# Conditioning products in halves for each head, and the second block's narrow heads in plain float32

## The chip, the cores and the metric

One core of one Trainium2 chip runs the whole program in one launch. Its engines are TensorE (matrix products), VectorE, ScalarE, GpSimd and the DMA queues. The metric is the device time of the core in microseconds (us), median over runs.

## The reference

The network has two blocks, each of two layers, in float32. The program keeps the product of float32 matrices by splitting each operand into a high part (float32r, a reduced format that TensorE reads in one pass) and a low part that holds the rest.

```python
def first_block(...):                    # 256 tokens, 256 context tokens, width 1024
    sc, sc_ctx = silu(c), silu(c_ctx)
    for l in range(2):                   # shift, scale, gate = split(sc @ w_ada + b_ada, 3)
        x, ctx = hybrid_layer(...)       # mlstm (4 heads), diff attention (8 heads), fourier; then merge

def second_block(...):
    for i in range(2):
        h = rms_norm(x, g_mix[i])
        x = x + (mixer_ab(h, ...) if i % 2 == 0 else mixer_cd(h, ...))
        x = x + memory_cross_attention(rms_norm(x, g_xq[i]), rms_norm(mem, g_mem[i]), ...)
        x = x + swiglu(rms_norm(x, g_ffn[i]), w_gate_up[i], w_down[i])
    return rms_norm(x, g_final)
```

mixer_ab has two attentions of 8 query and 2 key heads of 64 (normed and rotated; the second with a window and a sink). mixer_cd has one with 8 heads, 96 wide in scores and 64 in values (from low-rank projections), and a neighbourhood attention of 8 heads of 64 with a bias.

## The kernel before

Weights come in pieces of 512 KB. `weights` loads a piece on the sync queue into one of three `w_raw` buffers; ScalarE casts it to `w_high` (line 256); VectorE or GpSimd subtracts to give `w_low` (line 257), three buffers each. A product of split operands, `mm3`, is three float32r products, high by high, low by high and high by low (lines 262 to 264). Data are split in the same way: `split` (lines 270 and 271, or 273 and 274 with a scale), `stack_q` and `stack_k` (279 to 287), which lay the two parts of a 64-row operand one above the other in 128 rows, so that two products do (`mm_stacked`, 303 and 304).

The table `POOL` says, for each part of the program, which low parts of weights GpSimd makes: (1, 0), as for `ab`, is all of them, (3, 1), as for `cd`, each third, (0, 0) none.

The first block (to 1663 us of the profile) works on 512 tokens, in the later stages of layer 1 on 256. It is built in a block whose instruction order on every engine is set by a simulated timeline. In it stand the conditioning products sc @ w_ada: eight groups of 512 columns, `ada_product`, each with four raw pieces and eight plain float32 products of 32 stationary columns (line 510) into four column groups of one bank, the first four starting the sum and the last four ending it. Their pieces come through the same three `w_raw` buffers and the same queue as the weights. They stand behind heads 1 and 3 of the mlstm in both layers, and behind each pair of heads of the second attention in layer 0.

The second block's order is that in which the code is written, with the framework's filling in of work that is ready: mixer_ab (from 1663 us) does the key and value projection, two query projections (`tok_wide`, four pieces each), norm and rotation on VectorE (lines 330 to 348 and 1330 to 1348), transposes (1394, 1426), then for four pairs of heads and two kinds the scores, the softmax (`softmax_t`: maximum 1279, exponential 1286, scaling 1299, transposes 1301, split `p` 270 and 271) and the values (`pair_values`), which give `y` split again. The memory's keys and values (`memory_now`) for the cross attention are filled in between. The output projection (`residual`) follows. mixer_cd (from 2062 us) is made likewise with `near_project` for its second attention.

Of the kernel before, what the change touches and what calls it, by code (L numbers as in the profile page):

```python
# [30 lines left out]
SECOND = dict(load=2, act=16, q=8, p=4, x=4, e=3, s=2, t=3, r=2)  # L31
# [3 lines left out]
            merge0=(0, 0), merge1=(0, 0), t=(4, 2), e=(0, 0), ab=(1, 0), x=(3, 2), cd=(3, 1), f=(0, 0))  # L35
# [166 lines left out]
class Build:  # L202
# [97 lines left out]

    def mm_stacked(self, out, q, k, start=True, stop=True):
# [89 lines left out]
    def run(self):  # L391
        tc, nc = self.tc, self.nc
        with tc.tile_pool(name="sbuf", bufs=1) as base, \
# [19 lines left out]
            with tc.tile_pool(name="second", bufs=1, reuse_waits="tile") as self.pool, \  # L413
                    tc.tile_pool(name="psum2", bufs=1, space=PSUM) as self.ps:
                self.bufs, self.banks = SECOND, BANKS_2
                self.make_zeroed(4)
# [235 lines left out]
    def hybrid(self, l):  # L652
# [11 lines left out]
        for hd in range(4):  # L664
# [14 lines left out]
            if hd in (1, 3):  # L679
                self.ada_group(l, range(4 + hd // 2, 5 + hd // 2))  # L680
# [593 lines left out]
    def softmax_t(self, ps2, pts, qi, sink=None, row_scale=None):  # L1274
# [28 lines left out]
        if whole:  # L1303
# [62 lines left out]
    def mixer_ab(self, l):  # L1366
# [9 lines left out]
        for t in range(2):  # L1376
            kx = self.u("x")[:, :256]
            nc.scalar.activation(kx, pss[t][:, :256], AF.Copy, scale=r[:, t:t + 1])
            v = tuple(self.u("act", dt=F32R) for _ in range(2))
            vsrc = pss[t][:, 256:].rearrange("p (g c) -> p g c", c=64)  # L1380
            for dup in range(2):
                o = [x.rearrange("p (g u c) -> p g u c", u=2, c=64)[:, :, dup] for x in v]
                self.split(o[0], o[1], vsrc, scale=r[:, t:t + 1])
# [4 lines left out]
            kr = self.u("x")[:, :256]  # L1388
            kv = kr.rearrange("p (g c) -> p g c", c=64)
            self.rope_tok(kv[:, 0:2], ka, tab["r2_c"][:, t], tab["r2_s"][:, t], 2, 32)  # L1390
            self.rope_tok(kv[:, 2:4], kb, tab["r1_c"][:, t], tab["r1_s"][:, t], 2, 32)

            for g in range(4):
                nc.tensor.transpose((kt_ps, kt_ps2)[g // 2][:64, (g % 2) * S + t * P:(g % 2) * S + (t + 1) * P], kv[:, g], self.ident)
        kT = []
        for src in (kt_ps, kt_ps2):
            k = self.u("act", dt=F32R), self.zeroed()
            self.stack_k(k, src[:64])
            kT.append(k)
# [13 lines left out]
        for kind in range(2):  # L1413
# [14 lines left out]
            for i in range(2):  # L1428
                qT[kind].append([self.u("q", dt=F32R) for _ in range(2)])
                for u in range(2):  # L1430
                    self.stack_q(qT[kind][i][u], ptq[i][64 * u:64 * u + 64])
        for pr in range(4):
            for kind in range(2):
                g = pr // 2
                pts = self.new_pts()
                for qi in range(2):
                    ps = self.bank("sc").rearrange("p (u c) -> p u c", u=2)
                    qsl = slice((pr % 2) * S + qi * P, (pr % 2) * S + (qi + 1) * P)
                    ksl = slice(g * S, (g + 1) * S)
# [6 lines left out]
                def vs(u, s, g=g, kind=kind):  # L1446
                    lo = (2 * kind + g) * P
                    return tuple(x[:, lo:lo + 64 * (u + 1)] for x in vv[s])

                self.pair_values(y, 4 * kind + pr, pts, vs)  # L1450
# [3 lines left out]
    def near_project(self, pr, rb):  # L1454

        qk = []
        for j in range(2):
            w = self.weights("w_in_cd_2", 0, 0, KT, _cols(416 + 512 * j + P * pr, P))
            ps = self.feat(w, 0, self.h, 0, S)
            t = self.u("x")[:, :S]  # L1460
            self.nc.vector.tensor_tensor(t, ps, rb, op=ALU.mult)
            for u in range(2):
                if j == 0:
                    q = self.u("q", dt=F32R)[:, :S]
                    self.stack_q(q, t[64 * u:64 * u + 64])
                    qk.append(q)
                else:
                    k = self.u("q", dt=F32R)[:, :S], self.zeroed()[:, :S]
                    self.stack_k(k, t[64 * u:64 * u + 64])
                    qk.append(k)  # L1470
        return qk

    def mixer_cd(self, l):
# [5 lines left out]
        def values():  # L1479
            pss = self.tok_wide(arr, 0, h, _cols(416 + 1024, 512))  # L1480
            vd = []
            for t in range(2):
                v = tuple(self.u("act", dt=F32R) for _ in range(2))
                self.split(v[0], v[1], pss[t], scale=r[:, t:t + 1])
# [4 lines left out]
        for lo, n, gain in ((0, 2, "g_cq"), (256, 1, "g_ckv")):  # L1489
# [9 lines left out]
            c = tuple(self.u("p", [P, 2, S], F32R) for _ in range(2))  # L1499
# [42 lines left out]
        for t in range(2):  # L1542
# [7 lines left out]
            v = tuple(self.u("act", dt=F32R) for _ in range(2))  # L1550
            self.split(v[0], v[1], ps)
            vc.append(v)
        y = self.new_y2()
        for pr in range(4):
            pair = []
            for u in range(2):
# [8 lines left out]
            pts = self.new_pts()  # L1565
            for qi in range(2):
                ps = self.bank("sc").rearrange("p (u c) -> p u c", u=2)
                for u in range(2):
                    a, b = pair[u]
                    qsl = slice(qi * P, (qi + 1) * P)  # L1570
                    self.mm3(ps[:, u], (a[:, 0, qsl], b[:, 0, qsl]), (a[:, 1], b[:, 1]), True, True)
                self.softmax_t(ps, pts, qi)
            self.pair_values(y, pr, pts, lambda u, s, pr=pr: tuple(x[:, P * pr:P * pr + 64 * (u + 1)] for x in vc[s]))

            pts = self.new_pts()
            for qi in range(2):
# [11 lines left out]
            self.pair_values(y, 4 + pr, pts, lambda u, s, pr=pr: tuple(x[:, P * pr:P * pr + 64 * (u + 1)] for x in vd[s]))  # L1588
# [46 lines left out]
    def ffn(self, l):  # L1635
# [4 lines left out]
        for f in range(NF):  # L1640
# [11 lines left out]
            a = self.u("act" if f < 16 else "q", [P, 2, S], F32R)  # L1652
# [106 lines left out]
```

## Time and profile before

| | us |
|---|---|
| median of 3 runs | 2439.83 (2437.66 to 2440.39) |
| profiled execution | 2442.6 |
| its span | 2440.8 |
| TensorE busy | 2296.8 (94%) |
| VectorE busy | 1617.7 (66%) |
| ScalarE busy | 1163.4 (48%) |
| GpSimd busy | 472.2 (19%) |

The mean granted TensorE clock is 0.977 of full speed. A product's row shows it from its start to its end, and the next one starts before that end; what a product costs is read from the starts of two that follow each other.

### The profile page before, as it was taken

The page shows a single profiled execution, that of the slowest core. Times are in us where ns is not written, and L with a number is a line of the kernel's source. Part 1 is how long each engine was busy: PE and PEld are TensorE (multiplying, and loading weights), DVE is VectorE, ACT ScalarE, POOL GpSimd, SP SyncE. Part 2 cuts the span into 40 slices and gives each one's busy share as a digit, 9 for nine tenths or more (in the row PEclk, how much of TensorE's full clock was granted, in tenths as well). Part 3 has the DMA queues.
Part 4 walks back from the last instruction along what each step waited for, and adds up shares of the span by engine and source line. Part 5 has one row for each costly group of instructions (what it writes and reads, how often), then busy time and mean ns, then how long its engine had stood idle before and what let it go on. Part 6 is the DMA issues. An engine that isn't in the chain of part 4 may idle for free.

```text
span 2440.8 us, 40377 instructions
## 1 busy us (share of the span) xinstructions
PE 2296.8 (94%) x15566; PEld 2066.6 (85%) x15566; DVE 1617.7 (66%) x3372; ACT 1163.4 (48%) x2172; POOL 472.2 (19%) x354
## 2 busy tenths in 40 slices
PE   6999999999999999989999999898698999888998
PEld 3787878798797887779889999896588999788998
DVE  5745566466575555586557778666987766887765
ACT  3344443444554233335445666444465444665543
POOL 2422220111121102002110000123352211222221
PEclk8999999999999999999999999998899999999999
DMA  6223234323323434443445434554233555433554
GB/s 254 78 92 114 95 109 155 125 88 101 116 93 131 151 103 154 142 130 117 134 147 186 131 113 141 180 166 147 86 102 123 183 183 180 132 109 121 189 183 139
DMA packets 111072, 330.87 MB, mean 136 GB/s; under 512 B 12320, under 2 KB 24352, under 8 KB 110880
## 3 DMA queue, kind: packets, MB, share of 16 engines
q1 hardware_dynamic: 90432, 299.87, 37.5%
q10 hardware_dynamic: 20448, 28.42, 3.4%
q8 instruction: 123, 2.02, 0.4%
q14 instruction: 69, 0.57, 0.1%
HBM read 309.36 MB, written 18.87 MB: 134 GB/s over the span
## 4 chain that ended last, share of the span: by engine, by line
PE 80%; DVE 12%; ACT 3%; DMA 3%; issue 2%; POOL 0%; ACTq 0%; SPq 0%; DVEq 0%; POOLq 0%
PE mm L262 22%; PE mm L263 22%; PE mm L264 22%; PE pv L262 2%; PE pv L263 2%; PE pv L264 2%; DVE w_low L257 1%; DVE h L274 1%; ACT w_high L256 1%; DVE e L1299 1%; DMA w_raw<-wstream 1%; PE mm L510 1%; PE sc L303 1%; DVE mx L1279 1%; PE sc L304 1%
## 5 line engine op out<-in xcount | busy, mean ns | idle before, releaser
L256 ACT CAST w_high<-w_raw 128x1024 fp32r<-128x1024 f32 (+1 forms) x490 | 508.0, 1038 | 583.1 <-PE mm L263 351.8
L257 DVE TENSOR_TENSOR w_low<-w_raw,w_high 128x1024 fp32r<-128x1024 f32 (+1 forms) x395 | 497.3, 1260 | 189.3 <-ACT w_high L256 184.8
L262 PE MATMUL mm<-big,w_high 128*128 128x512 f32 (+1 forms) x1664 | 573.3, 346 | 12.4 <-DVE g L942 5.7
L263 PE MATMUL mm<-big,w_high 128*128 128x512 f32 (+1 forms) x1664 | 571.3, 344 | 0.0
L264 PE MATMUL mm<-big,w_low 128*128 128x512 f32 (+1 forms) x1664 | 570.0, 343 | 0.0
L257 POOL TENSOR_TENSOR w_low<-w_raw,w_high 128x1024 fp32r<-128x1024 f32 x95 | 230.4, 2428 | 739.6 <-ACT w_high L256 600.3
L262 PEld LDWEIGHTS mm<-big,w_high 128*128 128x128 f32 x1664 | 316.1, 190 | 56.6 <-DVE g L942 6.1
L264 PEld LDWEIGHTS mm<-big,w_low 128*128 128x128 f32 x1664 | 316.4, 190 | 37.5 <-DVE w_low L257 0.4
L263 PEld LDWEIGHTS mm<-big,w_high 128*128 128x128 f32 x1664 | 316.6, 190 | 36.5 <-DVE big L271 0.2
L263 PE MATMUL mm<-w_low,big 128*128 128x256 f32 x960 | 269.9, 282 | 4.2 <-POOL w_low L257 2.8
L262 PE MATMUL mm<-w_high,big 128*128 128x256 f32 x960 | 268.0, 282 | 1.6 <-ACT w_high L256 1.6
L264 PE MATMUL mm<-w_high,big 128*128 128x256 f32 x960 | 268.3, 281 | 0.0
L263 PE MATMUL mm<-h,w_high 128*128 128x256 f32 x896 | 255.5, 285 | 4.8 <-DVE h L274 4.1
L262 PE MATMUL mm<-h,w_high 128*128 128x256 f32 x896 | 253.4, 284 | 2.7 <-ACT h L273 1.7
L264 PE MATMUL mm<-h,w_low 128*128 128x256 f32 x896 | 253.6, 283 | 0.0
L263 PEld LDWEIGHTS mm<-w_low,big 128*128 128x128 f32 x960 | 181.1, 189 | 6.2 <-POOL w_low L257 3.7
L262 PEld LDWEIGHTS mm<-w_high,big 128*128 128x128 f32 x960 | 180.6, 189 | 3.5 <-ACT w_high L256 2.8
L264 PEld LDWEIGHTS mm<-w_high,big 128*128 128x128 f32 x960 | 181.0, 189 | 0.4
L263 PEld LDWEIGHTS mm<-h,w_high 128*128 128x128 f32 x896 | 169.7, 189 | 7.6 <-DVE h L274 7.5
L262 PEld LDWEIGHTS mm<-h,w_high 128*128 128x128 f32 x896 | 169.5, 190 | 4.4 <-ACT h L273 2.8
L264 PEld LDWEIGHTS mm<-h,w_low 128*128 128x128 f32 x896 | 169.7, 190 | 0.1
L1649 POOL TENSOR_TENSOR x<-x,r 128x256 f32<-128x256 f32 x44 | 60.2, 1368 | 190.7 <-ACT t L1648 190.7
(475 smaller groups left out, 4388.8 us busy)
## 6 DMA issues: line engine op xcount, KB each, us to landing
w_raw<-wstream SPq DMA_DIRECT2D x486, 512.0 KB, 3.4
w_raw<-wstream SPq DMA_DIRECT2D x32, 448.0 KB, 3.2
big<-wstream SPq DMA_DIRECT2D x16, 512.0 KB, 9.0
gates<-y ACTq DMA_DIRECT2D x24, 256.0 KB, 2.0
w<-gates SPq DMA_DIRECT2D x18, 256.0 KB, 3.8
load<-yacc ACTq DMA_DIRECT2D x16, 256.0 KB, 3.0
yacc<-w ACTq DMA_DIRECT2D x12, 256.0 KB, 2.0
gates<-y ACTq DMA_DIRECT2D x24, 128.0 KB, 1.8
```

Source lines behind the costliest of these rows:

```text
L256: nc.scalar.copy(h, raw)
L257: eng.tensor_tensor(lo, raw, h.bitcast(F32), op=ALU.subtract)
L262: nc.tensor.matmul(out, a[0], b[0], start=start, stop=False)
L263: nc.tensor.matmul(out, a[0], b[1], start=False, stop=False)
L264: nc.tensor.matmul(out, a[1], b[0], start=False, stop=stop)
L274: nc.vector.scalar_tensor_tensor(lo, src, scale, h.bitcast(F32), op0=ALU.mult, op1=ALU.subtract)
L303: nc.tensor.matmul(out, q, k[0], start=start, stop=False)
L304: nc.tensor.matmul(out, q, k[1], start=False, stop=stop)
L510: nc.tensor.matmul(ps[j:j + 32], self.sc32[:, 2 * q + k], raw[:, k], start=(q < 2), stop=(q >= 2))
L1279: nc.vector.reduce_max(mx, ps2, axis=AX.X, negate=True)
L1299: nc.vector.tensor_scalar(p[:, u], p[:, u], sm[:, u:u + 1], None, op0=ALU.mult)
L1649: nc.gpsimd.tensor_tensor(g, g, rb, op=ALU.mult)
```

## The change

The conditioning products are cut in two: `ada_half` loads two raw pieces and makes four products, one in each column group, each a sum of its own. The first half is copied to an SBUF buffer (`acc`) by ScalarE; in the second VectorE adds the buffer to the bank where ScalarE copied the bank. A half stands behind each head, sixteen in all. They have high priority, and the product that reads the last piece is put first, the other three behind it.

In the second block, scores and values of the heads of 64 and 96 are single plain float32 products. Queries, keys, probabilities and values there are not split; keys get two zero-padded tiles, one for each half of 128 rows, values stand between columns of zeros, so that both heads of a pair sum in one bank of 128 rows (four products for a pair where twelve were). `POOL` is (0, 0) for `ab` and `cd`: all low parts there are VectorE's. Buffers follow: `act` 8 for 16, four of `vz`, `p` 3 for 4.

```diff
-SECOND = dict(load=2, act=16, q=8, p=4, x=4, e=3, s=2, t=3, r=2)
+SECOND = dict(load=2, act=8, vz=4, q=8, p=3, x=4, e=3, s=2, t=3, r=2)
...
-            merge0=(0, 0), merge1=(0, 0), t=(4, 2), e=(0, 0), ab=(1, 0), x=(3, 2), cd=(3, 1), f=(0, 0))
+            merge0=(0, 0), merge1=(0, 0), t=(4, 2), e=(0, 0), ab=(0, 0), x=(3, 2), cd=(0, 0), f=(0, 0))
...
-    def ada_group(self, l, groups):
-        for g in groups:
-            self.ada_product(l, g)
...
-    def ada_product(self, l, g):
+    def ada_half(self, l, g, half):
 
         nc = self.nc
         ps = self.mm()
-        for q in range(4):
-            raw = self.raw_weights("w_ada", l, 2 * q, 2, _cols(512 * g, 512)).rearrange("p (k c) -> p k c", k=2)
-            for k in range(2):
-                j = 32 * (2 * (q % 2) + k)
-                nc.tensor.matmul(ps[j:j + 32], self.sc32[:, 2 * q + k], raw[:, k], start=(q < 2), stop=(q >= 2))
+        raw = [self.raw_weights("w_ada", l, 4 * half + 2 * q, 2, _cols(512 * g, 512)).rearrange("p (k c) -> p k c", k=2) for q in range(2)]
+
+        def product(j):
+            return nc.tensor.matmul(ps[32 * j:32 * j + 32], self.sc32[:, 4 * half + j], raw[j // 2][:, j % 2], start=True, stop=True)
+
+
+        with self.tc.high_priority():
+            first = product(3)
+            with self.tc.issue_after(first.ins if hasattr(first, "ins") else first):
+                for j in range(3):
+                    product(j)
+        if half == 0:
+            nc.scalar.copy(self.acc, ps)
+            return
         row = self.u("y")
-        nc.scalar.copy(row, ps)
+        nc.vector.tensor_tensor(row, ps, self.acc, op=ALU.add)
         pt = self.bank("tp")[:, :8]
...
-            if hd in (1, 3):
-                self.ada_group(l, range(4 + hd // 2, 5 + hd // 2))
+            self.ada_half(l, 4 + hd // 2, hd % 2)
...
+                if l == 0:
+                    self.ada_half(1, pair, u)
                 self.merge_gates(GATES_B)
-            if l == 0:
-                self.ada_group(1, range(pair, pair + 1))
...
+        if not isinstance(pts, tuple):
+            nc.scalar.copy(pts[:, :, :, sl], pt)
...
-    def pair_values(self, y, k, pts, vs):
-
-        po = self.bank("pv").rearrange("p (u c) -> p u c", u=2)
+    def between_zeros(self, n):
+
+        v = self.u("vz", [P, 64 * (2 * n + 1)])
+        self.nc.gpsimd.memset(v[:, :P * n].rearrange("p (g c) -> p g c", c=P)[:, :, :64], 0.0)
+        self.nc.gpsimd.memset(v[:, P * n:], 0.0)
+        return v, v[:, 64:].rearrange("p (g c) -> p g c", c=P)[:, :, :64]
+
+    def pair_values(self, y, k, pts, v, heads):
+
+        po = self.bank("pv")[:, :S]
         for u in range(2):
-            m = 64 * (u + 1)
+            lo = P * heads[u] + 64 * (1 - u)
             for s in range(2):
-                vh, vl = vs(u, s)
-                self.mm3(po[:m, u], (vh, vl), (pts[0][:, u, s], pts[1][:, u, s]), s == 0, s == 1)
-            rows = slice(64 * u, 64 * u + 64)
-            self.split(y[0][rows, k, :S], y[1][rows, k, :S], po[rows, u])
+                self.nc.tensor.matmul(po, v[s][:, lo:lo + P], pts[:, u, s], start=u == 0 and s == 0, stop=u == 1 and s == 1)
+        self.split(y[0][:, k, :S], y[1][:, k, :S], po)
...
-            v = tuple(self.u("act", dt=F32R) for _ in range(2))
-            vsrc = pss[t][:, 256:].rearrange("p (g c) -> p g c", c=64)
-            for dup in range(2):
-                o = [x.rearrange("p (g u c) -> p g u c", u=2, c=64)[:, :, dup] for x in v]
-                self.split(o[0], o[1], vsrc, scale=r[:, t:t + 1])
+            v, at = self.between_zeros(4)
+            nc.scalar.activation(at, pss[t][:, 256:].rearrange("p (g c) -> p g c", c=64), AF.Copy, scale=r[:, t:t + 1])
...
-                qT[kind].append([self.u("q", dt=F32R) for _ in range(2)])
-                for u in range(2):
-                    self.stack_q(qT[kind][i][u], ptq[i][64 * u:64 * u + 64])
+                qT[kind].append(self.u("q"))
+                nc.scalar.copy(qT[kind][i], ptq[i])
...
                     for u in range(2):
-                        self.mm_stacked(ps[:, u], qT[kind][pr // 2][u][:, qsl], tuple(x[:, ksl] for x in kT[kind]), kind == 0, kind == 0 or u == 1)
+                        nc.tensor.matmul(ps[:, u], qT[kind][pr // 2][:, qsl], kT[kind][g][u], start=kind == 0, stop=kind == 0 or u == 1)
...
+            if j == 0:
+                q = self.u("q")[:, :S]
+                self.nc.vector.tensor_tensor(q, ps, rb, op=ALU.mult)
+            else:
+                k = self.zeroed()
+                for u in range(2):
+                    sl = slice(64 * u, 64 * u + 64)
+                    self.nc.vector.tensor_tensor(k[u][sl], ps[sl], rb[sl], op=ALU.mult)
+        return q, k
...
-                a, b = (self.u("q", [P, 2, S], F32R)[:96] for _ in range(2))
-                self.split(a, b, pt)
-                pair.append((a, b))
-            pts = self.new_pts()
+                a = self.u("q", [P, 2, S])[:96]
+                nc.scalar.copy(a, pt)
+                pair.append(a)
...
-                    self.mm3(ps[:, u], (a[:, 0, qsl], b[:, 0, qsl]), (a[:, 1], b[:, 1]), True, True)
+                    nc.tensor.matmul(ps[:, u], pair[u][:, 0, qi * P:(qi + 1) * P], pair[u][:, 1], start=True, stop=True)
...
-                    self.mm_stacked(ps[:, u * S:(u + 1) * S], qk[u][:, qi * P:(qi + 1) * P], qk[2 + u])
+                    nc.tensor.matmul(ps[:, u * S:(u + 1) * S], qk[0][:, qi * P:(qi + 1) * P], qk[1][u], start=True, stop=True)
```

TensorE in the first block, around the group behind the first pair of heads of the second attention in layer 0; `big` and `sc_..<-k` are data of that attention, `w_raw` the conditioning weights. Before (the last pair of products, on the fourth piece, follows after four more score rows):

```order
L510 MATMUL mm_4436<-w_raw_4437,sc_13_97 32x512 x2
L510 MATMUL mm_4436<-w_raw_4441,sc_13_97 32x512 x2
L347 MATMUL tp_4089<-ones_64,e_4087 128x2 x4
L303 MATMUL sc_4208<-k_3627,q_3640 128x256
L304 MATMUL sc_4208<-kz_80,q_3640 128x256
L303 MATMUL sc_4213<-k_3631,q_3643 128x256
L1156 MATMUL tp_4199<-ident_62,e_4181 128x128 x2
L304 MATMUL sc_4213<-kz_74,q_3643 128x256
L510 MATMUL mm_4436<-w_raw_4445,sc_13_97 32x512 x2
```

After, the first half, behind the first head of that pair:

```order
L312 MATMUL sc_3944<-k_3611,q_3623 128x256
L313 MATMUL sc_3944<-kz_78,q_3623 128x256
L262 MATMUL mm_4063<-big_223,w_high_4059 128x512
L514 MATMUL mm_4114<-w_raw_4117,sc_13_97 32x512
L514 MATMUL mm_4114<-w_raw_4115,sc_13_97 32x512 x2
L514 MATMUL mm_4114<-w_raw_4117,sc_13_97 32x512
L263 MATMUL mm_4063<-big_224,w_high_4059 128x512
L264 MATMUL mm_4063<-big_223,w_low_4060 128x512
L262 MATMUL mm_4063<-big_223,w_high_4059 128x512
```

The products of a group stood in pairs, one for each piece, between other work; now the four of a half stand together, inside a projection's stream.

TensorE in mixer_ab, at the first scores of the second kind (`kz` are keys, `q` queries, `s` and `r` the window and the unit matrix, `mm` a projection of the memory). Before:

```order
L1426 MATMUL tp_18006<-ident_62,x_18009 128x128 x2
L1426 MATMUL tp_18005<-ident_62,x_18022 128x128 x2
L1426 MATMUL tp_18006<-ident_62,x_18022 128x128 x2
L1441 MATMUL sc_18108<-s_17769,r_17767 128x512
L303 MATMUL sc_18108<-act_17762,q_18033 128x256
L304 MATMUL sc_18108<-kz_17562,q_18033 128x256
L263 MATMUL mm_18620<-h_18581,w_high_18616 128x256
L264 MATMUL mm_18620<-h_18581,w_low_18617 128x256
```

After, with the values (`pv`) of a pair behind them:

```order
L1461 MATMUL sc_18102<-s_17797,r_17795 128x512
L1463 MATMUL sc_18102<-kz_17586,q_18053 128x256
L1314 MATMUL tp_18068<-ident_62,e_18064 128x128 x4
L1463 MATMUL sc_18102<-kz_17587,q_18053 128x256
L1314 MATMUL tp_18086<-ident_62,e_18082 128x128 x4
L1461 MATMUL sc_18126<-s_17797,r_17795 128x512
L1463 MATMUL sc_18126<-kz_17586,q_18053 128x256
L1463 MATMUL sc_18126<-kz_17587,q_18053 128x256
L1340 MATMUL pv_18094<-p_18057,vz_17692 128x256
L1340 MATMUL pv_18094<-p_18057,vz_17740 128x256
L1340 MATMUL pv_18094<-p_18057,vz_17692 128x256
L1340 MATMUL pv_18094<-p_18057,vz_17740 128x256
```

Two float32r products per score became one plain product, and the values of a pair are four products; the projections of the memory stand between them as before, with more of them ahead.

VectorE in mixer_ab, at the norm of the first keys (`hn`). Before:

```order
L274 SCALAR_TENSOR_TENSOR h_17568<-xres_17253,vecs_60,h_17568 128x256 x6
L274 SCALAR_TENSOR_TENSOR act_17669<-mm_17603,rstd_17588,act_17668 128x4x64
L1345 TENSOR_REDUCE hn_ss_17676<-t_17674 128x2
L334 TENSOR_SCALAR hn_r_v_17679<-hn_ss_17676 128x2
L335 TENSOR_SCALAR hn_r_y_17681<-hn_r_v_17679 128x2
L337 SCALAR_TENSOR_TENSOR hn_r_t_17680<-hn_r_y_17681 128x2
L338 TENSOR_TENSOR hn_r_t_17680<-hn_r_t_17680,hn_r_v_17679 128x2
L339 SCALAR_TENSOR_TENSOR hn_r_y_17681<-hn_r_t_17680,hn_r_y_17681 128x2
```

After:

```order
L274 SCALAR_TENSOR_TENSOR h_17592<-xres_17269,vecs_60,h_17592 128x256 x6
L257 TENSOR_TENSOR w_low_17668<-w_raw_17665,w_high_17667 128x1024
L257 TENSOR_TENSOR w_low_17808<-w_raw_17805,w_high_17807 128x1024
L257 TENSOR_TENSOR w_low_17826<-w_raw_17823,w_high_17825 128x1024
L1372 TENSOR_REDUCE hn_ss_17698<-t_17696 128x2
L343 TENSOR_SCALAR hn_r_v_17701<-hn_ss_17698 128x2
L344 TENSOR_SCALAR hn_r_y_17703<-hn_r_v_17701 128x2
L346 SCALAR_TENSOR_TENSOR hn_r_t_17702<-hn_r_y_17703 128x2
L347 TENSOR_TENSOR hn_r_t_17702<-hn_r_t_17702,hn_r_v_17701 128x2
L348 SCALAR_TENSOR_TENSOR hn_r_y_17703<-hn_r_t_17702,hn_r_y_17703 128x2
```

The split of the values (line 274 with `act`) is gone from there, and low parts of weights (257), which GpSimd made, stand ahead of the norm.

## Rows read from the trace of the kernel before

**Rows 1.** Engines busy, by stretch: first block; mixer_ab, its start; mixer_cd's attention.

```profile
core 0: us, PE busy (x) PEld busy (x) DVE busy (x) ACT busy (x) POOL busy (x), PEclk, DMA share, GB/s
0.00:1663.40 1663.40, 1589.75 (x10237) 1398.62 (x10237) 1053.48 (x2363) 756.27 (x1403) 270.64 (x222) 0.99 0.40 132
1663.40:1803.60 140.20, 107.97 (x552) 88.80 (x553) 113.36 (x259) 71.53 (x170) 48.13 (x21) 0.87 0.28 94
1663.40:1741.00 77.60, 56.62 (x224) 44.33 (x225) 57.03 (x127) 31.53 (x56) 28.99 (x12) 0.81 0.36 121
...
2106.00:2178.70 72.70, 61.16 (x442) 55.68 (x441) 59.89 (x119) 54.38 (x144) 15.41 (x9) 0.93 0.36 114
```

**Rows 2.** mixer_ab by line and shape: busy us, mean ns | idle before.

```profile
L257 POOL TENSOR_TENSOR w_low<-w_raw,w_high 128x1024 fp32r<-128x1024 f32 x19 | 45.6, 2402 | 96.0 <-ACT w_high L256 86.6 <-DMA load<-rpb 5.6 <-PE pv L264 3.8
L264 PE MATMUL mm<-w_high,h 128*128 128x512 f32 x64 | 28.9, 451 | 0.7 <-DVE h L274 0.7
...
L1299 DVE TENSOR_SCALAR e<-e,sm 128x256 f32<-128x256 f32 x32 | 20.1, 663 | 0.2
...
L1301 PE MATMUL tp<-ident,e 128*128 128x128 f32 x64 | 11.6, 289 | 10.1 <-DVE e L1299 10.1
...
L271 DVE TENSOR_TENSOR p<-tp,p 128x512 fp32r<-128x512 f32 x16 | 10.7, 682 | 1.4 <-ACT p L270 1.3
L264 PE MATMUL mm<-h,w_low 128*128 128x256 f32 x32 | 10.5, 334 | 0.0
...
L338 DVE TENSOR_TENSOR hn_r_t<-hn_r_t,hn_r_v 128x8 f32<-128x8 f32 x6 | 7.5, 1252 | 0.2
L338 DVE TENSOR_TENSOR hn_r_t<-hn_r_t,hn_r_v 128x2 f32<-128x2 f32 x6 | 7.4, 1236 | 0.2
```

**Rows 3.** Line 338, mixer_ab to 1741 us: ns min/median/max, first, last start.

```profile
L338 DVE TENSOR_TENSOR hn_r_t<-hn_r_t,hn_r_v x12: 160/1215/2356, 1682.0 to 1722.5; 128x2 f32<-128x2 f32 x6, 128x8 f32<-128x8 f32 x6
```

**Rows 4.** Line 1299 in mixer_ab's attention, same columns.

```profile
L1299 DVE TENSOR_SCALAR e<-e,sm x32: 339/347/2449, 1741.3 to 1797.0; 128x256 f32<-128x256 f32 x32
```

**Rows 5.** The chain that ended last, 200 to 1300 us: start us, us, what.

```profile
217.59 4.09 DMA w_raw<-wstream
...
332.15 1.84 PE mm L510 x12
...
560.70 1.02 PE mm L510 x8
```

**Rows 6.** Waits of TensorE, 200 to 1300 us.

```profile
PE mm L262 <- ACT w_high L256: 4.1, 5, 1.6
PE mm L510 <- DMA w_raw<-wstream: 3.9, 4, 1.6
...
PE mm L263 <- POOL w_low L257: 2.8, 2, 1.6
```

**Rows 7.** TensorE in order of time, mixer_cd's start: start us, us, name.

```profile
2067.05 0.68 PE L357 MATMUL tp<-ident,rstd 128*128 128x128 f32 x4 [0.15 <-DVE rstd L339]
2067.49 0.36 PE L262 MATMUL mm<-h,w_high 128*128 128x256 f32 x1
2067.69 0.28 PE L263 MATMUL mm<-h,w_high 128*128 128x256 f32 x1
2067.81 0.28 PE L264 MATMUL mm<-h,w_low 128*128 128x256 f32 x1
```

**Rows 8.** TensorE in order of time, an mlstm head of layer 1.

```profile
1187.35 0.69 PE L872 MATMUL sc<-negm,ident 4*128 4x256 f32 x2
```

**Rows 9.** mixer_cd's start, VectorE by line and shape (columns as Rows 2).

```profile
L257 DVE TENSOR_TENSOR w_low<-w_raw,w_high 128x1024 fp32r<-128x1024 f32 x6 | 7.3, 1222 | 1.4 <-ACT w_high L256 1.3
L338 DVE TENSOR_TENSOR rstd_t<-rstd_t,rstd_v 128x2 f32<-128x2 f32 x9 | 3.5, 392 | 0.2
```

**Rows 10.** mixer_cd's attention, by line and shape (columns as Rows 2).

```profile
L262 PE MATMUL mm<-h,w_high 128*128 128x256 f32 x48 | 14.0, 292 | 0.0
...
L262 PE MATMUL mm<-y,w_high 128*128 128x256 f32 x15 | 4.3, 314 | 0.5 <-ACT y L270 0.5
```

More of the change, by code (lines that the diff above doesn't have):

```diff
@@ L299, in make_zeroed, with make_zeroed_halves @@
             self.zero_tiles.append(t)
+    def make_zeroed_halves(self, n):
+        self.zero_tiles, self.n_zero = [], 0
+        for i in range(n):
+            t = [self.pool.tile([P, S], F32, tag=f"kz{i}{u}", name=self.name("kz"), bufs=1) for u in range(2)]
+            for u in range(2):
+                self.nc.gpsimd.memset(t[u][64 * (1 - u):64 * (2 - u)], 0.0)
+            self.zero_tiles.append(t)
     def mm_stacked(self, out, q, k, start=True, stop=True):
@@ L1302, in softmax_t @@
         sl = slice(qi * P, (qi + 1) * P)
-        if whole:
+        if not isinstance(pts, tuple):
+            nc.scalar.copy(pts[:, :, :, sl], pt)
+        elif whole:
             self.split(pts[0][:, :, :, sl], pts[1][:, :, :, sl], pt)
@@ L1310, in new_pts, with key_tile @@
         return tuple(self.u("p", [P, 2, 2, S], F32R) for _ in range(2))
-    def pair_values(self, y, k, pts, vs):
-        po = self.bank("pv").rearrange("p (u c) -> p u c", u=2)
+    def between_zeros(self, n):
[5 more added lines that the diff above has]
+        po = self.bank("pv")[:, :S]
         for u in range(2):
-            m = 64 * (u + 1)
+            lo = P * heads[u] + 64 * (1 - u)
             for s in range(2):
-                vh, vl = vs(u, s)
-                self.mm3(po[:m, u], (vh, vl), (pts[0][:, u, s], pts[1][:, u, s]), s == 0, s == 1)
-            rows = slice(64 * u, 64 * u + 64)
-            self.split(y[0][rows, k, :S], y[1][rows, k, :S], po[rows, u])
+                self.nc.tensor.matmul(po, v[s][:, lo:lo + P], pts[:, u, s], start=u == 0 and s == 0, stop=u == 1 and s == 1)
+        self.split(y[0][:, k, :S], y[1][:, k, :S], po)
+    def key_tile(self, src):
+        k = self.zeroed()
+        for u in range(2):
+            self.nc.scalar.copy(k[u][64 * u:64 * u + 64], src[64 * u:64 * u + 64])
+        return k
     def rope_tok(self, out, x, c, s, n, half):
@@ L1387, in mixer_ab @@
             self.head_norm(ka, 2, self.vec("g_ka"))
[L1388 to L1391, printed above, removed]
-            for g in range(4):
[L1394 to L1399, printed above, removed]
+            kr = self.u("x")
+            kv = kr.rearrange("p (g u c) -> p g u c", u=2, c=64)
+            for i, (kx_, rn) in enumerate(((ka, "r2"), (kb, "r1"))):
+                self.rope_tok([kv[:, 2 * i + g, 0].unsqueeze(1) for g in range(2)], kx_, tab[rn + "_c"][:, t], tab[rn + "_s"][:, t], 2, 32)
+                nc.scalar.copy(kv[:, 2 * i:2 * i + 2, 1], kv[:, 2 * i:2 * i + 2, 0])
+            for g in range(4):
+                nc.tensor.transpose((kt_ps, kt_ps2)[g // 2][:, (g % 2) * S + t * P:(g % 2) * S + (t + 1) * P], kr[:, P * g:P * g + P], self.ident)
+        kT = [[self.key_tile(src[:, g * S:(g + 1) * S]) for g in range(2)] for src in (kt_ps, kt_ps2)]
         y = self.new_y2()
@@ L1459, in near_project @@
             ps = self.feat(w, 0, self.h, 0, S)
[L1460 to L1471, printed above, removed]
+            if j == 0:
+                q = self.u("q")[:, :S]
+                self.nc.vector.tensor_tensor(q, ps, rb, op=ALU.mult)
+            else:
+                k = self.zeroed()
+                for u in range(2):
+                    sl = slice(64 * u, 64 * u + 64)
+                    self.nc.vector.tensor_tensor(k[u][sl], ps[sl], rb[sl], op=ALU.mult)
+        return q, k
     def mixer_cd(self, l):
@@ L1482, in values @@
             for t in range(2):
-                v = tuple(self.u("act", dt=F32R) for _ in range(2))
-                self.split(v[0], v[1], pss[t], scale=r[:, t:t + 1])
+                v, at = self.between_zeros(8)
+                nc.scalar.activation(at, pss[t].rearrange("p (g c) -> p g c", c=64), AF.Copy, scale=r[:, t:t + 1])
                 vd.append(v)
@@ L1498, in mixer_cd @@
             rc = self.rstd_rows(acc, S, n * P, by=96.0 if n == 2 else 1.0)
-            c = tuple(self.u("p", [P, 2, S], F32R) for _ in range(2))
+            c = tuple(self.u("q", [P, 2, S], F32R) for _ in range(2))
             self.norm_gain(c, raw, rc, [self.vec(gain, k) for k in range(n)], "t")
@@ L1549, in mixer_cd @@
             self.tok(ps, [(wv, 1)], ckv, t * P)
-            v = tuple(self.u("act", dt=F32R) for _ in range(2))
-            self.split(v[0], v[1], ps)
+            v, at = self.between_zeros(8)
+            nc.scalar.copy(at, ps.rearrange("p (g c) -> p g c", c=64))
             vc.append(v)
@@ L1568, in mixer_cd @@
                 for u in range(2):
[L1569 to L1571 removed]
+                    nc.tensor.matmul(ps[:, u], pair[u][:, 0, qi * P:(qi + 1) * P], pair[u][:, 1], start=True, stop=True)
                 self.softmax_t(ps, pts, qi)
[L1573 to L1575 removed]
+            self.pair_values(y, pr, pts, vc, (2 * pr, 2 * pr + 1))
+            pts = self.u("p", [P, 2, 2, S])
             for qi in range(2):
@@ L1651, in ffn @@
             nc.vector.scalar_tensor_tensor(t, t, 0.5, pu, op0=ALU.mult, op1=ALU.mult)
-            a = self.u("act" if f < 16 else "q", [P, 2, S], F32R)
+            if f % 2 == 0 and f < 8:
+                two = self.u("vz", [P, 2, 2, S], F32R)
+            a = two[:, f % 2] if f < 8 else self.u("act" if f < 16 else "q", [P, 2, S], F32R)
             self.split(a[:, 0], a[:, 1], t)
```

14 lines of the change are left out of this document (5 added, 9 removed).

## Prediction

> **What bounds the kernel now.** First I read the page's table, then busy time by stretch. The first block is bound by TensorE: busy 1589.75 of 1663.40 us, 0.956, at a clock of 0.99 [rows 1]. Only the products themselves and the stalls between them are worth anything there. In mixer_ab nobody is full: of 140.2 us TensorE is busy 108, VectorE 113, and GpSimd 48 [rows 1]. Busy time overstates TensorE, since a product's row shows its whole passage; by start to start one float32r product of 256 columns costs 0.12 us (I use 0.117, so 0.234 for 512) [rows 7], and a float32 instruction of 128 columns, as a transpose is, 0.11 (four take 0.44 [rows 7]). Counted so, mixer_ab holds 64 times three products of 512 columns (44.9), 32 times three of 256 (11.2) [rows 2], and by the code 64 for scores (7.5), 96 for values (11.2), 88 transposes (9.7), 8 window products (1.9) and about 1 of small ones: 87.4 us of work in 140.2, a share of 0.62.
>
> What holds it is seen in the rows by line. GpSimd makes 19 low parts at 2402 ns, and two lines of VectorE are far longer than they are elsewhere: line 338, on 2 or 8 elements a row, has a shortest of 160 ns, and a longest of 2356 [rows 3]; its twelve take 14.9 us instead of 1.9 [rows 2]. Line 1299 has a median of 347 ns and a longest of 2449 [rows 4]; its 32 take 20.1 us instead of 11.1. The longest are each about one GpSimd subtraction long: the short operation sits out a low part. That is 22 us of VectorE's 113, and it lies on the chain: norm and rotation come before TensorE's transposes, and behind line 1299 TensorE waits 10.1 us [rows 2]. TensorE's clock is 0.81 in the first part [rows 1], where it stands idle most.
>
> mixer_cd's attention, 72.7 us, has 37 us for its projections, scores and values (48 projection steps [rows 10], 48 and 32 products for scores, 96 for values, all times 0.117, the projections times three), 10.6 of transposes, up to 5 of the output projection [rows 10], less some 2 that lie ahead of the stretch: about 51, a share of 0.70. VectorE is busy 59.9 and GpSimd 15.4 there.
>
> **Conditioning products.** A group's first six products take 1.84 us and its last two, like four in four column groups, 1.02 [rows 5]: 2.86. After, two times four: 2.04. Eight groups: 6.6 us less. Behind that come the stalls: a group's fourth piece finds no free buffer until the first product has run, so its load of 4.09 us comes late and is on the chain [rows 5], and the weights behind it come late in turn. From 200 to 1300 us TensorE waits 3.9 us for these loads, 4.1 for high parts and 2.8 for GpSimd's low parts [rows 6], 10.8 in all. With two pieces the half fits beside one weight piece in the three buffers, and the loads can go out ahead. Some of these waits have other reasons, and each half can still stop the queue, now sixteen times: I take three quarters, 8.1. Ends: 0 (the stops only move) and 10.8 plus the 6.6. The copy by ScalarE and VectorE's add in place of ScalarE's copy are one instruction each for 512 columns, like line 271's 682 ns [rows 2], 16 in all; VectorE is busy 1053 of 1663 us there, and covers them. Without cover they would be 11 us. **First block: 15 us less**; as a timeline decides the order there, any edit also moves other instructions, by a few us either way.
>
> **Plain float32 products.** The trace has none of this shape. Each is two instructions there. Four instructions of 128 columns take 0.44 us from start to start [rows 7], so a product of 256 would take 0.44; the ones with four stationary rows show 0.69 for 256 columns [rows 8], their tail in it. The conditioning ones give 1.02 for four of 512 side by side [rows 5]. Nearest are the first, full 128 rows one behind the other: 0.44, upper end 0.69, lower end that of the two float32r products, 0.234, which no row suggests. mixer_ab has 64 of them (32 scores, 32 values) for 160 float32r ones: 28.2 for 18.7, so TensorE's work rises to 96.9. mixer_cd has 64 for 176: 28.2 for 20.6, from 51 to 58.6.
>
> The Trainium skill, "FP8 and Floating Point Precision", section TensorE Precision Notes, counts true float32 as four passes through the array, where three products of split operands are three and stacked ones two; this speaks against the change. By it a product costs four times 0.117, 0.47, an estimate that lies by the row's 0.44, and the sum would give back 4 us more; the trace so far agrees with the rule to within that.
>
> **VectorE.** In mixer_ab it loses 16 low parts of `p` at 0.68 (10.9), the ten of queries and keys at the same 512 columns (6.8), 8 of 16 of `y` and the four of values (256 columns, half of it: 4.1): 21.8. It gains 19 low parts of weights at 1.22 [rows 9]: 23.2. Its 113.4 lose also the 22 of standing still: 92.8, under TensorE's 96.9. In mixer_cd it loses about as much (`p` 10.9, the 96-row queries and the stacks) and gains some three at 1.22. ScalarE, at 71.5 and 54.4 [rows 1], copies where it cast.
>
> **Where the low parts stand.** VectorE's row now has low parts ahead of the first keys' norm, and behind each stands the norm, the rotation and TensorE's transposes of the keys. Each needs its piece loaded and a `w_low` buffer freed by earlier products, so VectorE stops when TensorE is late. TensorE has the first queries' 48 products of 512 columns, 11 us, to do meanwhile; I count nothing beyond the share below. GpSimd's zero fills are new: by columns against its low parts (1024 in 2.40 us) 0.75 each in mixer_ab, 1.35 each in mixer_cd, 6.9 us in all. Hidden, since GpSimd's work is 45.6 us shorter; 6.9 if not.
>
> **The sum.** With VectorE below TensorE a stretch is TensorE's work over the share it reaches. That share is 0.62 and 0.70 now, and 0.956 busy in the first block. Halfway is 0.81; I take 0.86, a bit more, because projections of the memory or of the next pair can fill both. mixer_ab: 96.9 / 0.86 = 112.7, 27.5 less. mixer_cd's attention: 58.6 / 0.86 = 68.1, 4.6 less. At its start nine of line 338 take 3.5 us for 1.4 [rows 9], in front of norms that TensorE waits for: 2 less. With 15: 49.1. The profiled execution, 2442.6, becomes 2393.5; it stood 2.8 above the median of 2439.8, so **2390.7 us**.
>
> **Rivals.** (1) VectorE takes GpSimd's place: its low parts come in order between softmax steps, `w_low` is late for TensorE, and the stretches reach only 0.75. For it: 92.8 against 96.9 is close, and both now wait on one queue. Against: no operation is held for 2.4 us any more. mixer_ab 129.2 (11.0 less), mixer_cd 78.1 (5.4 more), start 2, first block 15: 22.6 less, 2417.2 us.
>
> (2) The halves give nothing: sixteen stops where eight were, each a load to wait for inside a projection's stream. For it: VectorE and TensorE there lose as much as the short products save if each stop costs 0.9 us; the longest wait for such a load is 1.6 [rows 6]. Against: the loads can be issued a piece earlier. 34.1 less, 2405.7 us.
>
> (3) Better: without GpSimd in the way the stretches come to 0.956. mixer_ab 101.4 (38.8 less), mixer_cd 61.3 (11.4 less), start 2, first block the whole 17.4: 69.6 less, 2370.2 us.
>
> (4) Slower: plain products cost twice, 0.88, as they would if TensorE's clock stood at the lower of its two levels (1.2 of 2.4 GHz) while they run. With c the price, the gain is 140.2 - (68.7 + 64c)/0.86 + 72.7 - (30.4 + 64c)/0.86 + 17 = 114.7 - 148.8c: nothing at c = 0.77, and at 0.88 a loss of 16.2, 2456.0 us. For it: the clock was 0.81 in mixer_ab's first part, and is granted by what TensorE does. Against: it was low beside idle time, which shrinks, and 0.99 in the dense block [rows 1]. At the upper bound of 0.69 there is still a gain of 12, 2427.8.
>
> That the change doesn't do what it says has little room: in the order GpSimd's low parts of mixer_ab are on VectorE, and the four products of a half follow each other.
>
> **Chances.** My case 0.50, (1) 0.17, (2) 0.12, (3) 0.12, (4) 0.05, and 0.04 for a mix that ends near nothing. A measurement of this kernel tells about 0.2%, 4.9 us, from no change. Faster 0.91, within 0.04, slower 0.05. The range takes in (1), (2), most of (3) and the price of 0.69: 2368 to 2427.
>
> **What would show it.** Right: mixer_ab's length about 113 us, line 338's counterpart at 160 ns throughout and 1299's at 347, values and scores 0.44 us apart with TensorE's clock near 1; the first block some 15 us shorter, with conditioning products in runs of eight instructions of about 1.0 us and no load of 4 us on the chain. Wrong: `w_low` by VectorE as what ends TensorE's waits in mixer_ab (1); waits for `w_raw` in front of the conditioning products sixteen times (2); plain products 0.7 us apart or more (4).

## The result, and the profile after

The changed kernel takes 2379.15 us (median of 4 runs, 2374.97 to 2380.25) for 2439.7: a ratio of 0.975, 95% interval 0.9733 to 0.9767, or 60.6 us less. 2390.7 was predicted, in 2368 to 2427. The profiled execution has a span of 2378.5 us for 2440.8. Divided at the same instructions (the products that open a square-sum, and the first of each output projection), its length falls mostly where the change was made:

| stretch | before | after | less | forecast |
|---|---|---|---|---|
| first block | 1663.4 | 1636.3 | 27.1 | 15 |
| mixer_ab up to its output | 140.2 | 121.5 | 18.7 | 27.5 |
| its output projection | 27.4 | 26.0 | 1.4 | 0 |
| mixer_cd | 137.4 | 123.7 | 13.7 | 6.6 |
| the rest (cross, ffn, end) | 472.4 | 471.0 | 1.4 | 0 |

Busy time of each engine after, for the first block, mixer_ab (whole, its first part, its attention) and mixer_cd; columns as in [rows 1]:

```profile
0.00:1636.30 1636.30, 1575.87 (x10236) 1392.62 (x10236) 1049.29 (x2371) 755.50 (x1403) 278.88 (x230) 0.99 0.41 134
1636.30:1757.80 121.50, 106.78 (x521) 86.55 (x522) 87.03 (x244) 66.89 (x164) 3.43 (x2) 0.92 0.32 109
1636.30:1697.00 60.70, 46.69 (x196) 36.15 (x197) 46.46 (x129) 29.52 (x55) 3.43 (x2) 0.85 0.51 173
1697.00:1757.80 60.80, 60.09 (x326) 50.41 (x327) 40.58 (x116) 37.38 (x111) 0.00 (x0) 0.98 0.14 44
...
2015.40:2139.10 123.70, 120.56 (x816) 108.45 (x814) 85.06 (x183) 78.17 (x177) 17.32 (x17) 1.00 0.44 140
```

TensorE's own busy time in the first block is 13.9 us less, and its idle time (span less busy) 13.2 less, than in [rows 1]. mixer_ab is divided here at its first score. That product starts at 1734.1 us in the kernel before, so the two parts were 70.7 and 69.5 us long; [rows 1] divides 7 us later. mixer_ab's attention is now full, 60.09 of 60.80; its first part is not, 46.69 of 60.70, at a clock of 0.85. mixer_cd is nearly full too, 120.56 of 123.70.

mixer_ab after, by line and shape, as [rows 2] (line 347 was 338, 1312 was 1299):

```profile
L257 DVE TENSOR_TENSOR w_low<-w_raw,w_high 128x1024 fp32r<-128x1024 f32 x19 | 23.2, 1223 | 11.8 <-ACT w_high L256 11.7
...
L1463 PE MATMUL sc<-kz,q 128*128 128x256 f32 x64 | 18.0, 395 | 0.0
L1340 PE MATMUL pv<-p,vz 128*128 128x256 f32 x64 | 15.4, 384 | 0.0
...
L1312 DVE TENSOR_SCALAR e<-e,sm 128x256 f32<-128x256 f32 x32 | 10.0, 350 | 0.4
...
L347 DVE TENSOR_TENSOR hn_r_t<-hn_r_t,hn_r_v 128x8 f32<-128x8 f32 x6 | 1.0, 165 | 0.2
...
L347 DVE TENSOR_TENSOR hn_r_t<-hn_r_t,hn_r_v 128x2 f32<-128x2 f32 x6 | 1.0, 160 | 0.2
```

The stretched operations are gone: line 347 takes 160 to 165 ns, line 1312 350. The low parts are VectorE's at 1223. What TensorE waits for there is no longer the softmax:

```profile
PE tp L1448 <- DVE x L1364: 8.6, 2, 4.8
...
PE tp L1314 <- DVE e L1312: 0.3, 1, 0.3
```

It is the rotation of the queries (line 1364) in the first part, and the 10.1 us behind the softmax [rows 2] have become 0.3. The price of a plain product, TensorE in order of time:

```profile
1706.15 1.89 PE L1340 MATMUL pv<-p,vz 128*128 128x256 f32 x8
1707.88 0.60 PE L1314 MATMUL tp<-ident,e 128*128 128x128 f32 x4
```

Four products of 256 columns, eight instructions, from start to start 1.73 us: 0.43 each. The conditioning halves, on the chain of the first block:

```profile
212.37 0.99 PE mm L514 x8
...
427.44 0.99 PE mm L514 x8
```

Each half is one run of eight instructions in 1.0 us. From 200 to 1300 us the chain before had four loads of `w_raw`, each within a group and 3.7 to 4.1 us long; [rows 5] shows the first. Now no load stands on it from 200 to 1100 us, and three come after (1106.63, 1113.05 and 1229.70, of 3.3 to 6.4 us), the last of them right behind the last half. With the halves alone (halves_only, below) there is none in all this stretch.

### The profile page after: what moved, and what is told of

Its sections match the earlier page's. It is cut to its first block, busy times and chain, and to the rows that moved or that the text cites. A ratio compares the mean times of both kernels' runs of the same rounds, so it can differ in the third digit from the quotient of the medians.

```text
span 2378.5 us, 40132 instructions
## 1 busy us (share of the span) xinstructions
PE 2278.1 (96%) x15486; PEld 2055.0 (86%) x15486; DVE 1562.6 (66%) x3332; ACT 1145.2 (48%) x2134; POOL 403.6 (17%) x336
## 4 chain that ended last, share of the span: by engine, by line
PE 85%; DVE 6%; ACT 3%; DMA 3%; issue 1%; POOL 1%; ACTq 0%; SPq 0%; DVEq 0%; POOLq 0%
PE mm L262 24%; PE mm L263 24%; PE mm L264 24%; PE pv L263 1%; PE pv L262 1%; DVE w_low L257 1%; PE pv L264 1%; ACT w_high L256 1%; PE pv L1340 1%; DMA w_raw<-wstream 1%; PE sc L312 1%; PE sc L313 1%; PE tp L366 1%; PE tp L1314 1%; PE tp L1169 1%
## 5 line engine op out<-in xcount | busy, mean ns | idle before, releaser
L257 DVE TENSOR_TENSOR w_low<-w_raw,w_high 128x1024 fp32r<-128x1024 f32 (+1 forms) x429 | 534.1, 1246 | 224.0 <-ACT w_high L256 220.6
L262 PE MATMUL mm<-big,w_high 128*128 128x512 f32 (+1 forms) x1664 | 573.5, 346 | 18.7 <-DVE g L955 7.5
L257 POOL TENSOR_TENSOR w_low<-w_raw,w_high 128x1024 fp32r<-128x1024 f32 x61 | 148.9, 2443 | 538.3 <-ACT w_high L256 453.0
L905 POOL TENSOR_TENSOR e<-e,s 128x256 f32<-128x256 f32 (+3 forms) x68 | 65.7, 979 | 180.6 <-ACT e L904 180.3
```

The source lines that it names most:

```text
L257: eng.tensor_tensor(lo, raw, h.bitcast(F32), op=ALU.subtract)
L262: nc.tensor.matmul(out, a[0], b[0], start=start, stop=False)
L905: nc.gpsimd.tensor_tensor(e, e, place(sc, s, lo, hi), op=ALU.mult)
```

## The experiments

Each time is a median, with its ratio to the kernel before on the same chip and the 95% interval. The kernel before took 2438.1 to 2440.1 us there, so a difference between two changed kernels can have up to 2 us of the chip in it. "mixer_ab" is its length up to the output projection, "with output" the length to the next stage.

**Which part gives what.** The parts of the change by themselves. halves_only is the kernel before with `ada_half` and its calls, heads_only the changed kernel with `ada_group`, `ada_product` and their calls. low_parts_only is the kernel before with this line alone; plain_only is heads_only with the line turned back:

```diff
-            merge0=(0, 0), merge1=(0, 0), t=(4, 2), e=(0, 0), ab=(1, 0), x=(3, 2), cd=(3, 1), f=(0, 0))
+            merge0=(0, 0), merge1=(0, 0), t=(4, 2), e=(0, 0), ab=(0, 0), x=(3, 2), cd=(0, 0), f=(0, 0))
```

> The first block with conditioning products in halves, the second block as before. Theory: the parts add up, and this one is worth what the first block lost between the two traces, 1663.4 to 1636.3 us: 27 us less, about 2413 us. Rival (the prediction's term): the halves themselves save 15 us and the rest is chance of the order that the timeline made together with the other edits: about 2425 us.

Measured 2409.34 us, 0.9884 (0.9864 to 0.9905): 29.3 less. Its first block ends at 1635.0 us, as in the changed kernel (1636.3). The theory holds, the forecast's 15 does not.

> The second block with plain float32 heads and all its low parts on VectorE, the first block with its old groups. Theory: 33 to 35 us less (mixer_ab with its output 20, mixer_cd 14), about 2405 us, with mixer_ab 121 us long and its first part waiting for the rotation on VectorE. Rival: part of the second block's gain came from the first block's end (GpSimd and the queues in another state), and only some 25 us show.

Measured 2403.1 us, 0.9857 (0.9838 to 0.9876): 35.6 less, mixer_ab 121.1 us. The two parts add up (0.9884 times 0.9857 is 0.974; together they gave 0.975).

> Only the table: low parts of mixer_ab and mixer_cd on VectorE, split float32r heads as before. Theory: the stretched VectorE operations are gone (line 338 at 160 ns), but VectorE keeps all its splits and gets 23 us of low parts: mixer_ab about 125 us (15 less), mixer_cd 2 less, together about 2423 us. Rival: GpSimd was all of it, and this alone gives the whole 34 us of the second block, about 2406 us.

Measured 2408.86 us, 0.9885 (0.9861 to 0.9908): 29.8 less, close to the rival's 2406; mixer_ab came to 114.2 us, far below the 125 of the theory.

> Only the plain float32 heads in the second block, with the old table (mixer_ab's low parts all on GpSimd, each third in mixer_cd). Theory: splits gone, stretching kept: mixer_ab about 130 us (10 less), mixer_cd 8 to 10 less, about 2421 us. Rival: plain products cost TensorE 17 us more and give nothing by themselves: 2435 to 2450 us.

Measured 2426.63 us, 0.995 (0.9933 to 0.9967): 12.1 less, nearer to the theory, but nearly all from mixer_cd. By stage, with output, one trace each (split heads: the kernel before and low_parts_only; plain heads: plain_only and heads_only):

| | low parts on GpSimd | on VectorE |
|---|---|---|
| mixer_ab, heads split | 167.6 | 143.5 |
| mixer_ab, heads plain | 165.9 | 147.1 |
| mixer_cd, heads split | 137.4 | 131.8 |
| mixer_cd, heads plain | 127.2 | 123.3 |

In mixer_ab the table of low parts is the whole gain (24.1 us), and with it plain heads take 3.6 back; in mixer_cd the plain heads are most of it (8.5 to 10.2). With the table alone mixer_ab stands so:

```profile
1660.20:1774.40 114.20, 97.08 (x533) 79.85 (x534) 101.15 (x269) 69.20 (x166) 3.25 (x2) 0.91 0.32 112
...
1720.00:1774.40 54.40, 49.97 (x336) 43.26 (x335) 52.27 (x138) 40.45 (x118) 0.00 (x0) 0.98 0.13 43
```

VectorE is busy 101.15 of 114.20 us and TensorE 97.08; in the attention both are close to full, 52.27 and 49.97 of 54.40. Plain heads bring TensorE's 49.97 to 60.09, and the attention becomes 60.80 long.

**Is it GpSimd's instruction, or its late result?** The changed kernel with a subtraction on GpSimd for each of 25 pieces (eight of them the output projection's) into a tile that nobody reads; `idle` is that tile:

```diff
         eng.tensor_tensor(lo, raw, h.bitcast(F32), op=ALU.subtract)
+        if self.part == "ab" and h.shape[-1] == CW and self.idle is not None:
+            nc.gpsimd.tensor_tensor(self.idle, self.consts[:, :CW], h.bitcast(F32), op=ALU.subtract)
```

> The changed kernel, with GpSimd doing for each weight piece of mixer_ab a subtraction of the old size into a tile that nobody reads (one input is the piece's high part, so that it comes at the old time). Theory: GpSimd's subtraction itself holds VectorE's operations, whoever waits for its result: mixer_ab up to its output goes from 121 to about 138 us, the length with plain heads and GpSimd's low parts, total about 2396 us. Rival: what cost time was that low parts came late from GpSimd (2.40 us for 1.22); then nothing changes, 2377 to 2382 us.

Measured 2415.96 us, 0.9898 (0.9881 to 0.9914): 36.8 us more than the changed kernel, twice what was expected. mixer_ab is 150.2 us long for 121.5, its output 35.5 for 26.0. By line and shape, in mixer_ab (lines moved by 1 to 4), and then its two parts (columns as in [rows 1]):

```profile
L260 POOL TENSOR_TENSOR idle<-consts,w_high 128x1024 f32<-128x1024 f32 x19 | 55.6, 2925 | 112.7 <-ACT w_high L257 112.0
L258 DVE TENSOR_TENSOR w_low<-w_raw,w_high 128x1024 fp32r<-128x1024 f32 x18 | 30.2, 1682 | 6.6 <-ACT w_high L257 6.5
...
L350 DVE TENSOR_TENSOR hn_r_t<-hn_r_t,hn_r_v 128x2 f32<-128x2 f32 x6 | 7.5, 1248 | 0.2
```

```profile
1637.90:1722.60 84.70, 51.79 (x196) 40.28 (x196) 71.26 (x129) 29.66 (x54) 40.58 (x15) 0.74 0.37 124
1722.60:1788.20 65.60, 61.88 (x327) 51.28 (x327) 48.85 (x114) 37.52 (x111) 15.39 (x6) 0.97 0.09 33
```

Nobody is seen to wait for line 260, and line 350 is again at 1248 ns, VectorE's low parts at 1682 for 1223, GpSimd's at 2925 for 2402 [rows 2]: each holds the other. The scaling 1316 is held once in 32 (2435 ns, the others at most 355).

So the mechanism that the forecast read from [rows 3, 4] is shown, without a late result, and above all in the first part: 84.7 us for 60.7, with VectorE busy 71.26 for 46.46. The attention is 65.6 us for 60.8. With GpSimd's real low parts and plain heads (plain_only) it is 70.8, so there the unread subtraction gives back half; whether the other half is the late result was not tried.

The Trainium skill, "SBUF — State Buffer", section Who interferes with whom, has it that VectorE's operations with two SBUF inputs and GpSimd's that read SBUF exclude each other for a whole instruction, and that reductions are never held. This run agrees on the first: 1248 ns for line 350. On the second the trace of the kernel before agrees: three reductions there ran wholly inside one of GpSimd's subtractions (line 1345 at 1680.65 and 1706.01 us, line 1279 at 1771.73) and took 277, 686 and 660 ns, as the others of their size did.

**Back to split heads in mixer_ab.** Two kernels from the changed one. In ab_split mixer_ab's queries, keys, values and `p` are split as before, in ab_scores_split only queries and keys (keys, and in the first the values and a low part of `p`, lie in `vz` buffers). Both have:

```diff
-                        nc.tensor.matmul(ps[:, u], qT[kind][pr // 2][:, qsl], kT[kind][g][u], start=kind == 0, stop=kind == 0 or u == 1)
+                        self.mm_stacked(ps[:, u], qT[kind][pr // 2][u][:, qsl], tuple(x[:, ksl] for x in kT[kind]), kind == 0, kind == 0 or u == 1)
```

> The changed kernel with mixer_ab's heads split as before (low parts of weights on VectorE, mixer_cd plain, halves as changed). Theory: in mixer_ab plain products cost TensorE more than the splits cost VectorE; with split heads it was 3.6 us shorter (143.5 for 147.1 with its output), so about 2375.5 us. Rival: the parts are not additive there, and the time stays within 2 us of the changed kernel, 2377 to 2381.

Measured 2371.77 us, 0.972 (0.9705 to 0.9734): 7.4 us less than the changed kernel, whose interval just touches this one; mixer_ab with output is 143.6 for 147.5, as the table says.

> The changed kernel with mixer_ab's scores as two stacked float32r products as before, its values plain. Theory: this takes the dear splits (16 of p) off VectorE and gives TensorE only 2.7 us more than before: mixer_ab with its output about 142 us, 2373 to 2375 us. Rival: the first part of mixer_ab, which waits for the rotation, gets the splits of the queries back on its path and the gain is lost: 2379 us or more.

Measured 2369.22 us, 0.971 (0.9695 to 0.9724): 9.9 us less than the changed kernel; mixer_ab with output 138.9.

```profile
1633.80:1746.60 112.80, 101.58 (x520) 83.33 (x521) 90.46 (x250) 67.43 (x160) 3.62 (x2) 0.91 0.34 117
1692.70:1746.60 53.90, 53.63 (x320) 46.59 (x321) 42.80 (x122) 39.27 (x114) 0.00 (x0) 0.97 0.15 50
```

The attention is 53.9 us for 60.8, still full of TensorE: stacked scores are two products at 0.117 for one at 0.43. Plain values are the other way about: four at 0.43 for twelve at 0.117, a little more for TensorE, and no split of `p` for VectorE. That they pay rests on the stage (138.9 for 143.6, one trace each); the two times have intervals that overlap.

**What makes the halves worth it.** Two kernels from halves_only. halves_in_order:

```diff
-        with self.tc.high_priority():
-            first = product(3)
...
+        for j in range(4):
+            product(j)
```

halves_at_old_place, and the same behind a pair of heads of the second attention:

```diff
-            self.ada_half(l, 4 + hd // 2, hd % 2)
+            if hd in (1, 3):
+                for half in range(2):
+                    self.ada_half(l, 4 + hd // 2, half)
```

> Conditioning products in halves behind each head, but in the order of their pieces and without priority; second block as before. Theory: what the groups lost was the fourth piece without a buffer; halves alone cure it, so about 2410 us, as with priority. Rival: the four products standing together behind the last piece do it; without it products stand apart again, 0.4 us each pair and a wait for each piece: 2420 to 2430 us.

Measured 2414.96 us, 0.9897 (0.9882 to 0.9911): 25.2 less. The theory holds; the 4 us that order and priority seem to be worth are not told apart from nothing, as the two intervals overlap.

> Both halves of a group behind the second head, where the group stood; second block as before. Theory: what counts is that the two pieces of a half find buffers, wherever it stands: about 2410 us, as with a half behind each head. Rival: two halves in a row want four pieces close together again, the third and fourth wait as before, and half of the gain goes: 2420 to 2428 us.

Measured 2421.9 us, 0.9936 (0.9922 to 0.9951): 16.2 less. The rival: with two halves in a row loads are on the chain again.

```profile
329.07 1.07 PE mm L505 x8
330.53 6.44 DMA w_raw<-wstream
...
470.41 3.22 DMA w_raw<-wstream
...
553.80 3.36 DMA w_raw<-wstream
```

So of 29 us some 16 come from the halves as such, at the old place (7 of them are the shorter products, as shown below), and 13 from where the halves stand, with a head's work between them.

**Further with the same mechanism.** On ab_scores_split: cross_vector, by the line below; all_vector has (0, 0) in every entry of `POOL`.

```diff
-            merge0=(0, 0), merge1=(0, 0), t=(4, 2), e=(0, 0), ab=(0, 0), x=(3, 2), cd=(0, 0), f=(0, 0))
+            merge0=(0, 0), merge1=(0, 0), t=(4, 2), e=(0, 0), ab=(0, 0), x=(0, 0), cd=(0, 0), f=(0, 0))
```

> The fastest so far (halves, mixer_ab's scores split, its values and mixer_cd's heads plain), and the low parts of the two cross attentions, each third of them on GpSimd, on VectorE too. Theory: GpSimd's subtraction holds VectorE wherever TensorE waits for VectorE, which it does for some 2 to 3 us in a cross attention: 2 to 6 us less, 2363 to 2367 us. Rival: two of three are already VectorE's there, and the third adds work before the softmax: within 2 us, 2367 to 2371.

Measured 2362.47 us, 0.9684 (0.9668 to 0.9701): 6.8 us less than ab_scores_split. The chips differ by 2.1 us, and the intervals of the two ratios overlap a little; in the traces the two cross attentions are 40.4 us for 44.5 and 40.3 for 43.2.

> As cross_vector, with no low part on GpSimd anywhere, the first block's too. Theory: the first block is bound by TensorE, VectorE is busy 0.64 of it, and its low parts on GpSimd stand where VectorE was full; without them w_low comes late there: as cross_vector or up to 10 us slower, 2364 to 2376 us. Rival: they hold VectorE there as in mixer_ab, and the first block gets 10 us shorter or more, 2355 us or less.

Measured 2360.18 us, 0.9682 (0.9667 to 0.9696): not told apart from cross_vector by these intervals. In the first block GpSimd's low parts neither help nor harm by more than a few us. By its median this is the fastest version found, 19 us below the changed kernel, or 17 by the ratios.

## Why the prediction was right, and where its terms were off

**Range and direction** held. The sum was 49.1 us, 60.6 were measured; that it came so near is in part luck, since the errors of its terms, 12 and 7 us too little and 9 too much, partly cancel.

**Conditioning products: 15 us forecast, 27 to 29 measured.** The mechanism is shown (runs of eight in 1.0 us, and with the halves alone no load on the chain). In four traces with the old groups the first block is 1659.5 to 1663.4 us long, in six with the halves as in the change 1632.8 to 1637.9, some 26 less. Shorter products were right: 6.6 forecast, and TensorE was busy 23.9 us with the old ones and 17.1 with the new, 6.9 less. The term that was mis-sized is the stalls, 8.1 us, three quarters of three named waits [rows 6]. Of these 10.8 us 0.8 are left in the same stretch, 10.0 less, and all of TensorE's idle time fell by 13.2.

For the rest of the busy time, 7 us, the prediction had no term. The granted clock can be up to 3 of them: what it lacks of full speed, added over slices of 30 us, is 23.9 us in the first block before and 20.6 after. It rose around some groups (0.89 from 1170 to 1200 us before; 1.00 from 1150 to 1180 after) and fell elsewhere (from 300 to 330 us 1.00 before, 0.94 after). What the other 4 us are, the modelled ends of products among them, is open. Rival (2), no gain from halves, is refuted.

**Plain products: 0.44 us taken, 0.43 measured.** Right, and the clock in both attentions was near 1 (0.98 and 1.00), so rival (4) fell. By the four passes of the Trainium skill, "FP8 and Floating Point Precision", section TensorE Precision Notes, the estimate was 0.47; the measurement decides for 0.43.

**Sharing between VectorE and TensorE in mixer_ab: 27.5 forecast, 18.7 measured.** The lock was right in kind and size: lines 338 and 1299 took 35.0 us of VectorE [rows 2] and now take 12.0, 23 less where 22 were forecast. Wrong was the share that TensorE's work reaches: 0.86 was taken, and by the same count it came to 96.9 of 121.5, 0.80. No single share fits the stage. The attention is busy 0.99, more than rival (3)'s 0.956; the first part only 0.77, and TensorE waits 8.6 us there for the rotation. The prediction saw that low parts would stand ahead of the norm, and counted nothing for it beyond the share. How much of the wait they cause is not shown: TensorE waited for the rotation in the kernel before as well, 12.4 us up to the first score, for keys and queries. In the longest wait now, 4.8 us up to 1695.31, VectorE ends one low part and then does the norm and the rotation:

```profile
1690.44 1.75 DVE L1375 TENSOR_TENSOR x<-x,vecs 128x512 f32<-128x512 f32 x1
1692.22 1.70 DVE L1357 TENSOR_TENSOR t<-x,consts 128x256 f32<-128x256 f32 x2
```

Each takes about 1 us more than its like 13 us earlier (0.69 and 0.76), beside the only work of GpSimd that is left in the stage (line 1591, 3.43 us from 1689.88). So the lock seems to cost 2 us still. Rival (1)'s mechanism, TensorE waiting for `w_low`, is not among the named waits of the stage.

The prediction also gave up 21.8 us of VectorE's splits for 9.5 more of TensorE's work in mixer_ab, and that step had the wrong sign: once the lock was gone VectorE's splits were affordable, and TensorE's extra work set the end (147.1 us for 143.5 with split heads).

**mixer_cd: 6.6 forecast, 13.7 measured.** Up to the first score it gave 4.1 us for 2 forecast, behind it 9.6 for 4.6. There 0.86 was too low: TensorE is busy 0.97 of the stage, for 0.89 before. VectorE, freed of splits, no longer set its pace: TensorE's waits for its scaling (line 1299) and its splits (271), 5.9 and 3.7 us before, are 2.0 and none. With split heads the table alone gave 5.6, with plain ones 4.

## What to carry to other kernels

Ask first whether two engines slow each other by running at all: a tiny operation that sometimes lasts as long as the other engine's longest one is the sign, and in mixer_ab moving that work paid 24 us where the more visible change of precision cost 4. Weigh a trade of precision passes stage by stage, by the engine that is full there: it paid where a split cost VectorE much and TensorE little (values, low-rank heads), not where two stacked products did. Feed work that needs its own loads in portions that fit into the free buffers, with other work between the portions.

## What the runs showed of the hardware

An instruction of GpSimd whose result nobody reads cost 36.8 us in 25 executions, about 1.5 us each, half of its own 2.9. By stage, with output, that is 38.2 us (185.7 for 147.5), twice what GpSimd's real low parts cost there with plain heads (165.9 for 147.1), perhaps because VectorE had its own 1024-column subtractions to do beside it; that was not tried by itself.

TensorE's granted clock fell in some stretches with short stalls and not in others: in the kernel before it was 0.89 from 1170 to 1200 us, with named waits of 0.8 and 0.6 us, and 1.00 from 750 to 780, with waits of 1.5 and 0.7. So these traces give no rule by which a short stall costs more than itself.
